# Log-softmax over 50000 columns: loads and stores of a DMA-bound kernel moved from two queues into one, in turns

## The chip, the cores and the metric

The kernel runs on 1 core of one Trainium2 chip. The metric is the device time of one execution in microseconds; medians of several runs are given. A run that lies over 1.5% above the fastest of its kernel is counted as slow; all runs quoted are fast ones unless it is said.

A core has five engines that run instructions (TensorE, VectorE, ScalarE, GpSimd, SyncE) and 16 DMA engines that move data between HBM and the on-chip memory. A DMA issued here by SyncE or by ScalarE is cut into rows and dealt over all 16 DMA engines: the trace of the kernel before has 128 rows and 16 semaphore writes for each transfer. Each issuer has its own queue, q1 and q10 in the profile; a queue's work for one DMA engine is called its ring.

## The reference

```python
x = np.random.randn(16, 512, 50000).astype(np.float32)
max_x = np.max(x, axis=-1, keepdims=True)
shifted = x - max_x
log_sum_exp = np.log(np.sum(np.exp(shifted), axis=-1, keepdims=True))
return (shifted - log_sum_exp).astype(np.float32)
```

1638 MB are read and as many written, once each; the arithmetic is light.

## The kernel before

The 8192 rows are taken 16 at a time: 512 tiles of 128 partitions, where 8 partitions share a row and each holds 6250 numbers (25000 B). A tile is 3.2 MB and stays in one of 8 buffers from its load, through its computation, to its store. A round is 8 tiles. Each tile goes through VectorE (maximum over the partition, four small operations that combine 8 partitions), ScalarE (exponentials with their sums, in two instructions), TensorE (sums over 8 partitions), ScalarE (logarithm), and VectorE again (the subtraction, in place).

SyncE issues the loads. ScalarE issues the stores, each after the exponentials of the next tile:

```python
    @block.sync
    def _(sync):
        for j in range(NBUF):
            sync.dma_start(out=bufs[j], in_=dram(xq, 0, j)).then_inc(landed[j], 16)
        with sync.Fori(1, rounds) as q:
            for j in range(NBUF):
                take(sync, stored[j])          # wait until the buffer's store has landed
                sync.dma_start(out=bufs[j], in_=dram(xq, q, j)).then_inc(landed[j], 16)
        ...
    @block.scalar
    def _(scalar):
        ...
        def back(q, j):
            subtracted.next(                   # wait until VectorE has subtracted
                scalar.dma_start(out=dram(oq, q, j), in_=bufs[j])
            ).then_inc(stored[j], 16)
        ...
        with scalar.Fori(1, rounds) as q:
            last = q - 1
            for j in range(NBUF):
                front(j)                       # exponentials and logarithm of tile j
                back(q if j else last, (j - 1) % NBUF)
            settle()
```

## Time and profile before

| | kernel before |
|---|---|
| median time, 6 runs | 7618.52 us (7617.37 to 7620.07) |
| busy: VectorE, ScalarE, TensorE | 73%, 41%, 7% |
| DMA | 430 GB/s in the mean |

The page's busy digits are tenths of 40 equal slices of the span. The prediction shows the other lines, and uses a finer record, the 16 arrivals at a transfer's semaphore. They are called arrivals below too; a transfer has landed with the last of them.

### The profile page before, as it was taken

To read this page: it belongs to the slowest core of one execution; us is meant where nothing else is said; L and a number is where in the kernel's file an instruction comes from. 1 tells how busy PE (TensorE), PEld (TensorE's weight loads), DVE (VectorE), ACT (ScalarE), POOL (GpSimd) and SP (SyncE) were. 2 spreads that over 40 slices of the span, in tenths; PEclk is the share of its full clock that TensorE was granted. 3 is DMA by queue.
4 is the path that set the end of the run, shared out by engine and by line. 5 is a ranking of instruction groups with operands and counts; after the bars stand their busy time and mean duration, and the time that the engine had idled before them with its cause. 6 is when DMAs were issued, how large, how long until landed. Compare 5 with 4: busy or idle time off the path is not lost. (4 is left out here: it accounts for less than half of the span.)

```text
span 7617.7 us, 14954 instructions
## 1 busy us (share of the span) xinstructions
PE 519.0 (7%) x2048; PEld 475.1 (6%) x2048; DVE 5565.8 (73%) x3072; ACT 3153.3 (41%) x2561; POOL 1.2 (0%) x7
## 2 busy tenths in 40 slices
PE   0000000000000000000000000000000000000000
PEld 0000000000000000000000000000000000000000
DVE  7777777777777777777777777777777777777776
ACT  4444444444444444444444444444444444444443
POOL 0000000000000000000000000000000000000000
DMA  9999999999999999999999999999999999999998
GB/s 424 432 433 432 432 432 432 433 432 432 432 433 433 432 432 432 433 432 432 432 432 433 432 432 432 433 433 432 431 432 433 432 432 432 432 432 432 431 430 366
DMA packets 147459, 3276.88 MB, mean 430 GB/s; under 512 B 16385, under 2 KB 16385, under 8 KB 16385
## 3 DMA queue, kind: packets, MB, share of 16 engines
q1 hardware_dynamic: 73728, 1638.43, 50.0%
q10 hardware_dynamic: 73728, 1638.43, 50.0%
q14 instruction: 3, 0.02, 0.0%
HBM read 1638.40 MB, written 1638.40 MB: 430 GB/s over the span
## 5 line engine op out<-in xcount | busy, mean ns | idle before, releaser
L143 DVE TENSOR_REDUCE pmax<-buf 128x1 f32<-128x6250 f32 x512 | 3411.5, 6663 | 1960.6 <-DVEq L43 1960.6
L190 ACT ACTIVATE dump<-buf,negmax 128x3125 f32<-128x3125 f32 x1024 | 2938.2, 2869 | 3878.6 <-DVE negmax L160 3862.1
L164 DVE TENSOR_SCALAR buf<-buf,negmax,logsum 128x6250 f32<-128x6250 f32 x512 | 1789.4, 3495 | 3.9 <-ACT logsum L197 3.9
L227 PE MATMUL rowsum<-part,ones 128*128 128x1 f32 x2048 | 519.0, 357 | 7078.5 <-ACT dump L190 7078.5
L227 PEld LDWEIGHTS rowsum<-part,ones 128*128 128x128 f32 x2048 | 475.1, 322 | 7122.2 <-ACT dump L190 7122.2
L197 ACT ACTIVATE logsum<-rowsum 128x1 f32<-128x1 f32 x512 | 87.6, 171 | 564.8 <-PE rowsum L227 564.8
L190 ACT ACTIVATION_READ_ACCUMULATOR dump<-buf,negmax 128x1 f32 x1024 | 190.8, 186 | 0.0
L160 DVE STREAM_TRANSPOSE negmax<-spread 128x32 f32<-128x32 f32 x512 | 108.3, 212 | 17.7
L146 DVE STREAM_TRANSPOSE allmax<-pmax 128x32 f32<-128x32 f32 x512 | 108.3, 211 | 17.6
L149 DVE TENSOR_REDUCE rowmax<-allmax 128x4 f32<-128x32 f32 x512 | 95.1, 186 | 17.7
L155 DVE COPY spread<-rowmax 128x32 f32<-128x32 f32 x512 | 92.5, 181 | 17.8
L209 ACT ACT_TABLE_LOAD x1 | 1.3, 1283 | 1.0 <-SPq L90 1.0
L119 POOL TENSOR_SCALAR_AFFINE_SELECT ones<-ones 128x128 f32<-128x128 f32 x1 | 0.4, 403 | 0.1
L123 POOL TENSOR_SCALAR_AFFINE_SELECT ones<-ones 128x128 f32<-128x128 f32 x1 | 0.4, 397 | 0.1
L118 POOL MEMSET ones<- 128x128 f32 x1 | 0.2, 204 | 0.5 <-SPq L90 0.5
L254 POOL MEMSET const-bfloat16-1.0<- 128x1 bf16 x1 | 0.1, 101 | 0.0
L254 POOL MEMSET const-uint8-127<- 128x1 uint8 x1 | 0.1, 101 | 0.0
L254 POOL MEMSET const-float32-0.0<- 128x1 f32 x1 | 0.1, 98 | 0.3 <-issue 0.3
L254 POOL MEMSET const-float32-1.0<- 128x1 f32 x1 | 0.1, 98 | 0.0
## 6 DMA issues: line engine op xcount, KB each, us to landing
buf<-in_x_dram SPq DMA_DIRECT2D x512, 3125.0 KB, 51.8
out_dram<-buf ACTq DMA_DIRECT2D x512, 3125.0 KB, 37.0
```

Source lines behind the costliest of these rows:

```text
L119: gpsimd.affine_select(out=ones3, in_=ones3, pattern=[[-G, R], [0, G]], base=0, channel_multiplier=1, compare_op=ALU.is_ge, fill=0.0,).wai ...
L123: gpsimd.affine_select(out=ones3, in_=ones3, pattern=[[G, R], [0, G]], base=G - 1, channel_multiplier=-1, compare_op=ALU.is_ge, fill=0.0,) ...
L143: vector.reduce_max(out=pmax, in_=bufs[j], axis=AX).then_inc(on_dve.sem)
L146: vector.transpose(out=allmax, in_=pmax.to_broadcast([P, SQ]))
L149: vector.tensor_reduce(out=rowmax, in_=allmax.rearrange("p (r g) -> p r g", g=G), op=ALU.max, axis=AX, negate=True,)
L155: vector.tensor_copy(out=spread.rearrange("p (r g) -> p r g", g=G), in_=rowmax[:, :, None].to_broadcast([P, SQ // G, G]),)
L160: on_dve.next(vector.transpose(out=shift[j], in_=spread)).then_inc(shifted.sem)
L164: vector.tensor_scalar(out=bufs[j], in0=bufs[j], scalar1=shift[j][:, 0:1], scalar2=logs[j], op0=ALU.add, op1=ALU.subtract,)
L190: ins = scalar.activation(out=dump, in_=bufs[j][:, c * EXP_C : (c + 1) * EXP_C], func=ACT.Exp, bias=shift[j][:, 0:1], scale=1.0, accum_out ...
L197: scalar.activation(out=logs[j], in_=rowsum[:, j : j + 1], func=ACT.Ln)
L209: nc.scalar.preload_act_table_set("natural_log_exp_and_others")
L227: ins = tensor.matmul(rowsum[:, j : j + 1], ones, parts[j][:, c : c + 1], start=c == 0, stop=c == nexp - 1,)
```

## The change

The intent: one queue for everything. SyncE issues a store, then a load, then a store, so that loads and stores take turns by whole transfers. Three other stores stand between a buffer's store and the load that fills it again, so that the wait for that store should be over by the time SyncE comes to it. ScalarE is rid of DMA.

```diff
+    LEAD = 3
     @block.sync
     def _(sync):
+        def load(j, src):
+            sync.dma_start(out=bufs[j], in_=src).then_inc(landed[j], 16)
+        def store(j, dst):
+            subtracted.next(sync.dma_start(out=dst, in_=bufs[j])).then_inc(stored[j], 16)
         for j in range(NBUF):
-            sync.dma_start(out=bufs[j], in_=dram(xq, 0, j)).then_inc(landed[j], 16)
+            load(j, dram(xq, 0, j))
+        for j in range(LEAD):
+            store(j, dram(oq, 0, j))
+        subtracted.settle(sync)
         with sync.Fori(1, rounds) as q:
+            last = q - 1
             for j in range(NBUF):
+                k = (j + LEAD) % NBUF
+                store(k, dram(oq, last if k >= LEAD else q, k))
                 take(sync, stored[j])
-                sync.dma_start(out=bufs[j], in_=dram(xq, q, j)).then_inc(landed[j], 16)
+                load(j, dram(xq, q, j))
+            subtracted.settle(sync)
+        for j in range(LEAD, NBUF):
+            store(j, dram(oq, rounds - 1, j))
     ... (ScalarE: back() and its calls removed; its loop now runs from round 0)
```

More of the change, by code (lines that the diff above doesn't have):

```diff
@@ L198, in front @@
             ).then_inc(logged.sem)
-        def back(q, j):
-            subtracted.next(
-                scalar.dma_start(out=dram(oq, q, j), in_=bufs[j])
-            ).then_inc(stored[j], 16)
         def settle():
-            for count in (on_act, shifted, added, subtracted):
+            for count in (on_act, shifted, added):
                 count.settle(scalar)
         nc.scalar.preload_act_table_set("natural_log_exp_and_others")
-        for j in range(NBUF):
-            front(j)
-            if j:
-                back(0, j - 1)
-        settle()
-        with scalar.Fori(1, rounds) as q:
-            last = q - 1
+        with scalar.Fori(0, rounds):
             for j in range(NBUF):
                 front(j)
-                back(q if j else last, (j - 1) % NBUF)
             settle()
-        back(rounds - 1, NBUF - 1)
     @block.tensor
```

## The prediction

> **What bounds the kernel now.** I read the page first, then the stretches at the start and the end, then the timeline of the middle, and last the landing records of single transfers. From the page of the kernel before, the DMA row, the rate row, the queues, and the issues:
>
> ```profile
> DVE  7777777777777777777777777777777777777776
> ACT  4444444444444444444444444444444444444443
> DMA  9999999999999999999999999999999999999998
> GB/s 424 432 433 432 432 432 432 433 432 432 432 433 433 432 432 432 433 432 432 432 432 433 432 432 432 433 433 432 431 432 433 432 432 432 432 432 432 431 430 366
> ...
> q1 hardware_dynamic: 73728, 1638.43, 50.0%
> q10 hardware_dynamic: 73728, 1638.43, 50.0%
> ...
> buf<-in_x_dram SPq DMA_DIRECT2D x512, 3125.0 KB, 51.8
> out_dram<-buf ACTq DMA_DIRECT2D x512, 3125.0 KB, 37.0
> ```
>
> The reader is to see that the 16 DMA engines are full in every slice but the last, that VectorE and ScalarE are not, and that loads (queue q1, from SyncE) and stores (q10, from ScalarE) each take half of the DMA time. A load takes 51.8 us to land and a store 37.0 us, though 3.2 MB at 432 GB/s is 7.4 us: they stand in backlogs, which says that the engines never look for work.
>
> The middle of the kernel (timeline) shows the period of one tile:
>
> ```profile
> 3806.29 6.66 DVE L143 TENSOR_REDUCE pmax<-buf 128x1 f32<-128x6250 f32 x1 [3.84 <-DVEq L43]
> 3806.35 0.34 ACTq L202 DMA_DIRECT2D out_dram<-buf  x1
> ...
> 3821.17 6.66 DVE L143 TENSOR_REDUCE pmax<-buf 128x1 f32<-128x6250 f32 x1 [3.87 <-DVEq L43]
> ```
>
> One tile per 14.88 us here; VectorE works 11.0 us of it (6.66 maximum, 0.9 four small operations, 3.50 subtraction) and waits 3.8 us for its load's landing.
>
> The end looks as if it held a gain. In stretches of 5 us (columns: stretch, its us, the five engines' busy time, clock, DMA share, GB/s):
>
> ```profile
> 7545.00:7550.00 5.00, 0.00 (x0) 0.00 (x0) 4.00 (x5) 4.25 (x3) 0.00 (x0) 1.00 0.96 415
> 7550.00:7555.00 5.00, 1.01 (x4) 0.93 (x4) 2.04 (x1) 1.91 (x3) 0.00 (x0) 1.00 0.42 175
> 7555.00:7560.00 5.00, 0.00 (x0) 0.00 (x0) 4.93 (x3) 0.00 (x0) 0.00 (x0) 1.00 0.95 405
> 7560.00:7565.00 5.00, 0.00 (x0) 0.00 (x0) 3.90 (x4) 4.38 (x3) 0.00 (x0) 1.00 0.23 100
> ```
>
> From 7550 us on the mean share falls to about half, yet VectorE still gets its last tiles only at 7567.8 and 7582.7 us. The share is a mean over 16 engines, so I looked at the 16 arrivals that each transfer's semaphore records, one for each DMA engine. Of the last load, 15 arrive from 7543.9 to 7545.8 us and one at 7582.7. That one falls behind steadily: 1.1 us behind the median in round 3 (a round is 8 tiles), 10.0 in round 21, 18.6 in round 39, 37.5 in round 63. From round 3 to 63 the last arrival advances by 118.94 us a round, so 7.434 us a transfer; the median of the others, from round 3 to 39, by 118.46 us, 7.404 a transfer. **One slow DMA engine bounds the kernel.** Its first load lands at 11.26 us and its last store at 7616.46; 7605.2 us over the 1023 transfers between is 7.434 each, its steady pace. So it has no hole, not even in the tail; the holes are those of the 15 others. In the records a row of 25000 B takes 928 ns in the median and a semaphore write 9 ns: 8 x 928 + 9 = 7433 ns, the slow engine's pace with no gap.
>
> **What the Trainium skill says.** All from "DMA: Bandwidth & Descriptors". "Issuing engines are not separate DMA queues" says that transfers from SyncE and ScalarE run on the same 16 DMA engines and interleave, so that spreading saves only sequencer time. The trace agrees: both queues have 50.0%. "Queues, rings and completion order" says that each issuer has one ring on each DMA engine, that an engine takes turns between rings packet by packet, and that within a ring descriptors are consumed in order. Hence the change replaces alternation by row with alternation by whole transfer. The trace agrees as far as it can: while both queues are full, each takes twice the 7.43 us per transfer. "Why a DMA increments its semaphore by 16 and not by 1" says that the participating engines each post their own arrival; this is what I used above, and the 16 arrivals are there. "Bandwidth", under "Where 436 GB/s comes from", puts the ceiling at 435.2 GB/s. An estimate from that page: 3276.88 MB / 435.2 GB/s = 7529.6 us, 1.2% under the present time. The trace never holds more than 433 in a slice.
>
> **The change, part by part.**
>
> Bytes, transfers and rows are unchanged: 512 loads and 512 stores, 128 rows of 25000 B each.
>
> ScalarE loses 512 issues of 0.34 us, 174 us of its sequencer, and a wait for the subtraction. It is 41% busy and not the bound: worth 0. A store is no longer held until ScalarE is done with the next tile. In the middle, the subtraction that starts at 3813.81 us ends at 3817.31, its store goes out at 3821.18: 3.9 us earlier now. With a backlog in the ring that shortens no transfer: 0.
>
> SyncE gains those issues: two of about 0.33 us in 14.87 us. Worth 0, unless its order blocks it. Its queue is now store of tile n (five turns after its load), load, store, load. In slots of 7.43 us, a load in slot 1 has its store in slot 10, so 8 slots or 59.5 us lie between the load's end and its store's start. What must fit: the landing (about 1.4 us, as the second-last store took 8.8 us from issue to landing for 7.4 us of data); the next load 14.87; its maximum and small operations 7.5; the subtraction 3.5; about 1.5 for issue and first data. That is 29 us of 59.5. In the other direction, a load waits for a store with six transfers behind that store in the ring: 44.6 us of work, against about 3 us for the receipt and the new issue; even where the store before it waited for its subtraction, the load reaches the ring about 5 slots, 37 us, ahead. So the ring never runs dry, and the buffers are not the bound.
>
> The pace in one ring is the open term. The four first loads, alone in their ring, land at 11.26, 18.65, 26.05 and 33.51 us: 7.417 us each, semaphore included, and the late engine falls no further behind in them (0.39 us throughout). The two last stores, also back to back in one ring, land 7.43 us apart (7606.49 and 7613.92 in the median). So neither load after load nor store after store opens a hole for the completion write. A load and a store together make 14.847 us, 7.4235 in the mean. The sum, if changing direction costs nothing: 11.3 to the first landing + 1023 x 7.4235 = 7594.3, + 1.2 from the last landing to the end = 7606.8 us, 11 us less than now.
>
> **The rivals.**
>
> Nothing moves: the late engine is slow in itself, and keeps 7.434 us. Then 11.3 + 1023 x 7.434 + 1.2 = 7617.5 us. For it: it is one engine, always behind. Against it: it did not fall behind while only loads ran, though over 22 us I would see only 0.09 us.
>
> The late engine is slow because of taking turns, and one ring cures it: all go at 7.404, and it is 11.3 + 7574.3 + 1.2 = 7587 us. For it: the loads alone. Against it: the 15 others take the same turns without loss.
>
> The slow engine's extra 0.03 us comes on top of the pace of unmixed transfers: 1023 x 0.03 = 31 us on 7606.8, 7638 us.
>
> A new hole: with one ring an engine has nothing else to do while a transfer's completion is ordered behind its last write or its direction changes. Each 0.05 us in each of 1024 transfers is 51 us: 7658 us with that. Being over 2% slower (152 us) needs 0.15 us a transfer. For it: before, the other ring stood ready just there, and no place of this trace has a load and a store in turns in one ring. Against it: the two pairs of equal kind have no hole.
>
> A dry ring: the wait for another store blocks SyncE, with a ready store behind it. Half a slot lost per tile would be 512 x 3.7 = 1900 us. The 37 us of slack speak against it.
>
> **Range and chances.** I take the middle between "nothing moves" and "pace of unmixed transfers": 7612 us. The cured engine sets the low end, 7582 with a little margin; the high end holds a hole of 0.05 us: 7662. Faster by over 2% would be below 7466 us, under the 7529.6 of the page's ceiling: 0.01. Slower by over 2% needs the hole of 0.15 us or a dry ring, which the trace of before can't exclude: 0.04. Within 2%: 0.95.
>
> **What would show it right or wrong.** The changed profile should have one hardware queue with about 100% of the DMA share; the DMA row at 9 and about 432 GB/s through the middle; VectorE waiting on landings for some 3.8 us per tile; no more 0.34 us issues on ScalarE; a tile period of 14.80 to 14.90 us. Loads should take about 45 us to land or less, stores about 40: in one ring each waits its turn. If the last arrival still falls 0.48 us a round behind the others, the slow engine is slow in itself; if it stays with them, taking turns was to blame. The prediction is wrong if the DMA share sinks in the middle, if rows take visibly over 928 ns or holes follow the 4 B semaphore writes, or if SyncE's wait for a subtraction ends long after the ring is dry.

## The result

| | before | changed |
|---|---|---|
| median of 6 runs | 7618.52 us | 7639.27 us (7638.04 to 7640.7) |
| ratio | | 1.0027, 95% interval 1.0014 to 1.004 |
| span of the profiled run | 7617.7 us | 7637.1 us |

The changed kernel is 0.3% slower: small, but 21 us, where the six runs of each kernel lie within 3 us.

From the page of the changed kernel, the lines that answer to those of before:

```profile
DVE  7777777777777777777777777777777777777776
ACT  4344444444444444444444444444444444444443
DMA  9999999999999999999999999999999999999998
GB/s 419 429 430 431 431 430 431 430 431 431 431 431 431 431 431 431 431 431 431 431 431 431 431 431 431 431 431 431 431 431 431 431 431 431 431 431 431 431 431 371
...
q1 hardware_dynamic: 147456, 3276.87, 100.0%
...
buf<-in_x_dram SPq DMA_DIRECT2D x512, 3125.0 KB, 47.8
out_dram<-buf SPq DMA_DIRECT2D x512, 3125.0 KB, 41.0
```

One hardware queue now has all of the DMA time. The engines are as full as they were, yet the rate is 431 where it was 432 or 433, and 419 to 430 in the first slices. So the time did not go into idle DMA engines: the same rows take longer.

The timeline of the middle:

```profile
3810.20 0.34 SPq L139 DMA_DIRECT2D out_dram<-buf  x1
3810.80 0.35 SPq L136 DMA_DIRECT2D buf<-in_x_dram  x1
...
3814.05 6.66 DVE L163 TENSOR_REDUCE pmax<-buf 128x1 f32<-128x6250 f32 x1 [3.87 <-DVEq L43]
...
3828.93 6.66 DVE L163 TENSOR_REDUCE pmax<-buf 128x1 f32<-128x6250 f32 x1 [3.87 <-DVEq L43]
```

The store is issued as soon as its subtraction ends, the load 0.6 us after it, and VectorE waits for its landing as long as before. The wait of SyncE for the older store costs nothing that can be seen: of the 0.6 us the store's own issue takes 0.34. Over the whole run that wait is 32.8 us; the lines are shown at e4.

The end, in stretches of 5 us as before:

```profile
7565.00:7570.00 5.00, 1.01 (x4) 0.93 (x4) 1.97 (x1) 1.99 (x3) 0.00 (x0) 1.00 0.98 420
7570.00:7575.00 5.00, 0.00 (x0) 0.00 (x0) 4.93 (x3) 0.00 (x0) 0.00 (x0) 1.00 1.01 435
7575.00:7580.00 5.00, 0.00 (x0) 0.00 (x0) 3.97 (x4) 4.31 (x3) 0.00 (x0) 1.00 0.76 325
...
7625.00:7630.00 5.00, 0.00 (x0) 0.00 (x0) 0.00 (x0) 0.00 (x0) 0.00 (x0) 1.00 0.06 25
```

DMA share 0.06 is one engine of 16: the slow one works alone from 7625 us on, at the very end. Its last load arrives at 7598.26 us, and its five last stores at 7605.75, 7613.27, 7620.81, 7628.27 and 7635.74, without a hole. (Arrivals are given from the start of the span, as in the profile. The prediction's are 0.15 us later throughout, which changes none of its differences.)

The arrivals give the account. I take the pace in us for a load and a store together, from the loads of buffer 0 over whole rounds; "median" is the median of the 16 DMA engines, "last" the latest of the 16:

| kernel, rounds | median engine | last engine |
|---|---|---|
| before, 20 to 40 | 14.807 | 14.867 |
| changed, 1 to 8 | 14.901 | 14.947 |
| changed, 20 to 40 | 14.850 | 14.898 |

In rounds 1 to 8 of the changed kernel the buffers differ, from 14.908 to 14.947 on the last engine; from round 20 on they agree.

On the last engine, the first load to the last store took 7616.31 - 11.11 = 7605.2 us before and 7635.74 - 11.09 = 7624.65 us after: 19.45 us more, which is the 19.4 us by which the profiled spans differ. Load for load, the changed kernel is 1.8 us later in round 8 and then falls back by 0.24 us a round, to 15.0 us in round 63. The other 4 us show in the last stores: before, a store ran beside the last load and landed 4.0 us after it; now the first of the five stores that are left lands 7.5 us after it. In the row records the mean row of 25000 B went from 928.7 to 931.6 ns. Before, 96% of the rows took exactly 928 ns; after, 50% did, and most of the others 929 to 941.

The backlog is healthy. Taking, at each issue, the time until the transfer ahead of it in the ring has landed on the last engine, it is never under 33.2 us from the fourth round on, up to the last four stores, which wait for the computation and still find 11.4 us or more. So the ring does not run dry on the engine that bounds the kernel.

### The profile page after: what moved, and what is told of

Read it like the earlier page. It is cut to its first block, busy times and chain, and to the rows that moved or that the text cites. A ratio compares the mean times of both kernels' runs of the same rounds, so it can differ in the third digit from the quotient of the medians.

```text
span 7637.1 us, 14641 instructions
## 1 busy us (share of the span) xinstructions
PE 518.8 (7%) x2048; PEld 474.9 (6%) x2048; DVE 5566.3 (73%) x3072; ACT 3153.3 (41%) x2561; POOL 1.2 (0%) x7
## 6 DMA issues: line engine op xcount, KB each, us to landing
buf<-in_x_dram SPq DMA_DIRECT2D x512, 3125.0 KB, 47.8
```

## The experiments

The theories at the start. **Own pace**, later called **unmixed**: loads alone and stores alone have paces of their own, which are a little worse than both together, and the order in one ring makes each engine do one kind at a time. Rivals: **price of a change**, a small cost each time a ring changes direction; **one ring**, small holes in a ring that a second ring fills; and SyncE's waits.

### Loads alone, stores alone (e1, e2)

```diff
# e1: no compute; 8 stores at the end
-                k = (j + LEAD) % NBUF
-                store(k, dram(oq, last if k >= LEAD else q, k))
-                take(sync, stored[j])
+                take(sync, landed[j])
                 load(j, dram(xq, q, j))
# e2: no compute; 8 loads at the start
-                k = (j + LEAD) % NBUF
-                store(k, dram(oq, last if k >= LEAD else q, k))
                 take(sync, stored[j])
-                load(j, dram(xq, q, j))
+                store(j, dram(oq, q, j))
```

> 512 loads back to back in one ring, no compute, 8 stores at the end (output wrong on purpose). Theory 'own pace' (a direction left to itself has a pace of its own, and changing direction costs nothing): the 15 quick DMA engines take about 7.417 us a load, as the four first loads of the kernel before did; time 11.3 + 511 x 7.417 + 8 x 7.43 + 2 = 3863 us. Theory 'price of a change' (rows of one kind run as quickly as in the kernel before, and each change of direction in a ring costs some 20 ns): 7.404 us a load on the quick engines. If the slow engine is slow in itself, it falls behind by about 0.03 us a load here too, 15 us over the run, and the time is about 3878 us; if only taking turns with stores makes it slow, it stays level.

> 8 loads, then 512 stores back to back in one ring, no compute (output wrong on purpose). 'Own pace': about 7.432 us a store on the quick engines, so that load and store together make the 14.849 us that they take in the changed kernel (118.78 us a round / 8); time 11.3 + 519 x 7.43 + 2 = 3870 us, or 3885 with a slow engine. 'Price of a change': 7.404 us a store, and load and store together 14.81, the kernel before's.

Measured: e1 3868.9 us, e2 3900.0 us (2 runs each; outputs wrong). From the two pages, e1 first, then e2:

```profile
HBM read 1638.40 MB, written 25.60 MB: 430 GB/s over the span
```

```profile
HBM read 25.60 MB, written 1638.40 MB: 427 GB/s over the span
```

With an engine's whole time spent on one kind, the rates are 430 and 427 in spans that include start and end. The arrivals over rounds 20 to 40: a load takes 7.425 us on the median engine and 7.426 on the last; a store 7.447 on the median and 7.487 on the last. Together 14.872 and 14.913. The changed kernel has 14.850 and 14.898, the kernel before 14.807 and 14.867. So unmixed transfers are slower than mixed ones without any change of direction, which is what "own pace" says, by even more than the change lost. "Price of a change" foretold 7.404 us for each kind, and falls. "Own pace" was right in kind and too low in size: it had 7.417 and 7.432 us, and the times came out 6 us (e1) and 15 us (e2, with a slow engine) over its own.

A second thing: in e1 no engine falls behind (the last is 0.4 us behind the median in the last round), in e2 one does, by 0.040 us a store, 20 us at the end. **Left to one kind, an engine is slow in stores only.** Its 0.040 us would make most of the 0.05 to 0.06 us a tile that one engine loses in both whole kernels, if that is the same engine: the records don't number the engines.

The word "median" hides something in e2. The 16 engines have three paces there (rounds 20 to 60): eight take 7.438 us a store, seven 7.456, and one 7.487; 7.447 is only the middle between the first two groups. In e10 below, on another chip (the record has chip 4 for e2 and chip 10 for e10), the groups and their paces are the same within 0.001 us. So it is no fault of one chip. Why the engines fall into these groups is not shown.

### Two stores, then two loads (e3)

```diff
-            for j in range(NBUF):
-                k = (j + LEAD) % NBUF
-                store(k, dram(oq, last if k >= LEAD else q, k))
-                take(sync, stored[j])
-                load(j, dram(xq, q, j))
+            for j in range(0, NBUF, 2):
+                for i in (j, j + 1):
+                    k = (i + LEAD) % NBUF
+                    store(k, dram(oq, last if k >= LEAD else q, k))
+                for i in (j, j + 1):
+                    take(sync, stored[i])
+                    load(i, dram(xq, q, i))
```

> The changed kernel with two stores, then two loads in the ring instead of one and one: half as many changes of direction. 'Own pace': same as the changed kernel, 7639 us within 3. 'Price of a change': half of the 21 us comes back, about 7629 us.

Measured: 7720.17 us (7698.16 to 7735.3, 4 runs), ratio 1.0123. Neither theory foretold that. It goes against "price of a change" in sign, but "own pace" missed it too. The page shows when it happens:

```profile
GB/s 417 424 427 429 431 431 430 430 431 431 431 430 431 431 431 430 430 430 430 429 428 429 430 429 429 426 420 419 416 416 418 417 418 418 418 420 418 414 414 369
```

For some 4000 us it runs nearly at the changed kernel's pace (14.925 us a tile on the last engine in rounds 20 to 40), then drops to 15.32 in rounds 40 to 63. By then the slow engine is 22 us behind. SyncE can only reuse a buffer when the slow engine is done with it, and this order has less in the ring: the last engine's backlog at issue is 28 us in the median, and never under 22.7. The quick engines have that much less the lag. From round 50 on, 12% of the issues reach a median engine whose last transfer landed less than 2 us later, so it is dry or nearly so; in the changed kernel there is none before the last stores. Rows over 950 ns, 1119 in the changed kernel, are 6875 here. That the quick engines come to the edge of running dry is shown. Why the slow engine, with over 20 us of work in its ring, becomes slower at the same time is not, and so it is not shown either that the dryness costs the 1%.

### A shorter lead (e4)

```diff
-    LEAD = 3
+    LEAD = 1
```

> The changed kernel with one other store between a buffer's store and its next load instead of three. The ring's order by kind is the same; a load has 2 transfers (15 us) instead of 6 queued behind the store that it waits for. 'Own pace' and 'price of a change' both say 7639 us within 5. If instead SyncE's waits add to the time, as a third theory says, the shorter slack makes it clearly slower, 7660 us or more.

Measured: 7644.38 us (7641.51 to 7647.0, 4 runs), ratio 1.0032. That is 5 us more than the changed kernel, just over the 5 that were allowed, and the backlog went from 33 to 14.3 us at the least. In rounds 20 to 40 the last engine's pace is again 14.898 us, and the 5 us come from the start (15.085 in rounds 1 to 8 for buffer 0, against 14.947). What SyncE waited for changed altogether. Its waits for a store to land, first in the changed kernel, then in e4 (us in total, times, longest):

```profile
SPq L43 <- SPq L43: 32.8, 6, 8.3
```

```profile
SPq L43 <- SPq L43: 6981.0, 509, 30.1
```

Two hundred times the wait for 5 us: SyncE's waits are not the cause of the 21 us, and three stores of lead are more than enough. In rounds 20 to 40 the median engine, too, takes 14.896 us here, so the quick engines are held back to the slow one's pace, and the slow one loses nothing by it. Held-back quick engines alone do not explain e3.

### Smaller pieces, in one ring or two (e5 to e8)

```diff
# e5: each transfer as two of 64 rows, SyncE;  e7: as eight of 16 rows
-            sync.dma_start(out=bufs[j], in_=src).then_inc(landed[j], 16)
+            for h in PIECES:
+                sync.dma_start(out=bufs[j][h], in_=src[h]).then_inc(landed[j], 16)
# e6: rows 0 to 63 from SyncE, rows 64 to 127 from ScalarE, between its own work, loads four tiles ahead
# e8: store piece, load piece, store piece, load piece ... in one ring
```

> Control. The changed kernel with each transfer issued as two of 64 rows, both from SyncE, in the same order of kinds (two half stores, two half loads). Same rows, one more semaphore write of 9 ns for each half load and half store: 2 x 9 ns x 512 = 9 us. All theories: 7639 + 9 = 7648 us, within 8.

> As e5, but the second half of each transfer is issued from ScalarE: two rings in turns on each DMA engine, both of which hold stores and loads in the changed kernel's order, so an engine still has one kind at a time. Theory 'unmixed' (what the changed kernel loses is that an engine no longer has loads and stores in flight at once): as e5, within 8 us. Theory 'one ring' (a single ring has small holes that a second ring fills): the kernel before's pace, some 20 us under e5, about 7628 us.

> Control. The changed kernel with each transfer issued as eight of 16 rows, one row for each DMA engine, all eight of a store and then all eight of a load, from SyncE. 14 more semaphore writes of 9 ns per tile: 65 us. All theories: about 7704 us, or more if small transfers cost more than their semaphore write.

> As e7, but the 16-row stores and 16-row loads take turns one by one in the single ring: an engine changes direction after each row, as in the kernel before, with one ring as in the changed kernel. 'Unmixed': 15 to 20 us under e7. 'One ring': as e7. 'Price of a change', which e3 already speaks against: 16 times as many changes of 20 ns, more than 100 us over e7.

Measured, all with correct results, medians of 4 runs: e5 7742.99, e6 8985.21, e7 9120.21, e8 11981.92 us. (Two of e6's runs and one of e7's are counted as slow; e6's fast ones are 8835.45 and 8872.14 us.) The controls e5 and e7 missed their own numbers by 95 and 1416 us, so the four can't answer the question that they were made for. What went wrong is in the first stretches, where only loads run (columns as before; e5, then e7):

```profile
4.00:12.00 8.00, 0.00 (x0) 0.00 (x0) 0.00 (x0) 0.00 (x0) 0.00 (x0) 1.00 1.06 222
12.00:20.00 8.00, 0.00 (x0) 0.00 (x0) 0.43 (x1) 0.00 (x0) 0.00 (x0) 1.00 0.97 203
```

```profile
12.00:20.00 8.00, 0.00 (x0) 0.00 (x0) 0.00 (x0) 0.00 (x0) 0.00 (x0) 1.00 0.86 100
20.00:28.00 8.00, 0.00 (x0) 0.00 (x0) 0.00 (x0) 0.00 (x0) 0.00 (x0) 1.00 0.89 103
```

Loads of 64 rows run at half of the 432 GB/s of 128 rows, loads of 16 rows at a quarter. The Trainium skill, "SBUF — State Buffer", section "Door 1: The DMA port swizzle", says that the rate depends on how many of 16 ports the partitions reach, and by its table 64 consecutive partitions reach 8 and 16 consecutive ones 4. These rates agree with it. Later the DMA engines get out of step (in e5 the arrivals at one buffer spread over 9.0 us in the first round and 19.8 in the next) and e5 recovers to about 430 GB/s: its first slice of 40, at 248 GB/s, holds some 80 of the 95 us. But the pieces are spoilt as a test: I changed how the rows lie on the ports together with what I wanted to change. Little can be kept. The pair e7 and e8 has the same pieces, and taking turns row by row in one ring took 2862 us more than eight and eight. But with one and the same order e8 runs at 422 GB/s in one slice and at 217 in another, so no price of a single change of direction can be read from it. Why e6, with the pieces of e5 in two rings, took over 1000 us more than e5 is not explained either.

### One kind in two rings (e9, e10)

The clean form of the question whether the second ring matters: e1 and e2 again, whole transfers, dealt in turn to both queues.

```diff
+    @block.sync
+    def _(sync):
+        half(sync, range(0, NBUF, 2))      # the same loop, even tiles
+    @block.scalar
+    def _(scalar):
+        half(scalar, range(1, NBUF, 2))    # odd tiles
```

> e1 with the tiles dealt in turn to SyncE's and ScalarE's rings (512 loads, whole transfers, no compute, output wrong on purpose). Two rings in turns, but still one kind at a time. 'One ring': the rows go back to 928 ns, as they were with two rings in the kernel before, and a load takes 7.404 us instead of the 7.425 of e1: 11 us less than e1, about 3858 us. 'Unmixed': as e1, 3869 us within 4.

> e2 with the tiles dealt in turn to the two rings (512 stores, output wrong on purpose). 'One ring': the mean row falls from 934 to 928 or 929 ns and the time by 20 to 30 us, to about 3875 us. 'Unmixed': as e2, 3900 us within 5, with one engine still about 0.04 us a store behind the others.

Measured: e9 3868.09 us (e1 3868.9), e10 3900.3 us (e2 3900.0), 2 runs each. The pace on the median and the last engine is 7.425 and 7.425 us a load, 7.447 and 7.488 us a store; the mean rows are 931.1 and 934.1 ns, where they were 931.0 and 934.2. A second ring does nothing for transfers of one kind, though in e9 the row after a row on an engine always comes from the other queue. "One ring" falls; what the kernel before has and these have not is loads beside stores.

### Relieving the slow engine (e11)

```diff
# kernel before; tile 0 of rounds 8, 24, 40 and 56, and the matching wait for 32
-        scalar.dma_start(out=dst, in_=bufs[j]).then_inc(stored[j], 16)
+        scalar.dma_start(out=dst[:120], in_=bufs[j][:120]).then_inc(stored[j], 16)
+        scalar.dma_start(out=dst[120:], in_=bufs[j][120:]).then_inc(stored[j], 16)
```

The rule meant below is in "DMA: Bandwidth & Descriptors" of the Trainium skill, section "Why a DMA increments its semaphore by 16 and not by 1": a transfer issued by SyncE or ScalarE uses the largest number of engines up to 16 that divides its slowest dimension on both sides, and takes the lowest-numbered ones.

> The kernel before, except that in 4 of the 64 rounds one store is issued as 120 rows and 8 rows, which by the Trainium skill's rule on how many engines a transfer uses should leave out DMA engine 15 for the 120 (8 rows for each of 15 engines) and engines 8 to 15 for the 8. If the engine that falls behind is number 15, it is relieved of 4 x 8 rows, 29.7 us, of the 31 us that it falls behind in the whole run (512 x 0.06), the pace is that of the others, 14.807 us a tile, and the time is 11.3 + 512 x 14.807 + some 5 = about 7595 us, the first version under the kernel before. If it is one of 8 to 14, nothing changes (7618); if one of 0 to 7, it has 4 rows more, and it is 7622 us.

Measured: 7729.44 us (7637.59 to 7766.05, 6 runs, two of them counted as slow), ratio 1.0144; none of the three numbers came. The profiled run, 7637.59 us, is the best. The trace agrees with the rule on the number of engines: it has 28 semaphore writes more than the kernel before, 7 for each of the 4 split stores, as 15 + 8 - 16. In the stores of round 9, after the first such store, one engine arrives 16.5 us ahead of the median, and another is still 4.6 us behind and goes on falling behind, to 7.4 in round 15. So an engine was relieved, and not the one that falls behind. Besides, each such store costs something itself: the last engine's pace for the loads, 14.86 us in round 7, is 15.17 in round 9 and 15.74 in round 25. So if the page's numbering holds, the slow engine is not number 15; which one it is stays open, and so does the scatter of this version's runs.

### Both kinds in both rings (e12)

```diff
# even tiles: loads and stores from SyncE; odd tiles: from ScalarE; order in each ring as in the changed kernel
-    subtracted = Count(sem("subtracted"))
+    subtracted = [Count(sem("subtracted_even")), Count(sem("subtracted_odd"))]
...
+            store(k, dram(oq, last if k else q, k))   # SyncE, even k = j + 2
+            take(sync, stored[j])
+            load(j, dram(xq, q, j))
```

> The changed kernel's order by turns, but with the even tiles' loads and stores in SyncE's ring and the odd tiles' in ScalarE's (whole transfers; each ring has store, load, store, load, with one other store of its own between a buffer's store and its next load). Two rings, each of both kinds. 'One ring' (e9 and e10 speak against it): the kernel before's 7618 us within 5, whatever the phases. 'Unmixed': it depends on what stands beside what, which the landings will show. Where both rings hold the same kind at a time, the changed kernel's pace, 14.90 us a tile on the slow engine, 7637 us; where a store runs beside a load, the kernel before's 14.87 and 7620 us; a mixture lies between. A dry ring, which the shorter lead could bring, would show as rows over 950 ns and 7660 us or more.

Measured: one run of 7630.96 us, five of 7816.92 to 7846.13 us; the five are counted as slow by their distance from the first, and the profile is of that kind, with 10154 rows over 950 ns and the median engine 27 us ahead of the last. That looks like the dry ring of e3 again, on the quick engines, so the profile says nothing on the pace, and the single quick run, between the two kernels, has no trace. Inconclusive.

No version with right results beat the kernel before.

## Why the prediction was right, and where it was off

**The bound.** It named one slow DMA engine as what bounds the kernel, without a hole in its work. That held: the change in this engine's time from first to last arrival, 19.45 us, is the whole change of the span. In the changed kernel, too, the half-empty DMA row near the end is that of the quick engines.

One proof that it offered does not hold. "8 x 928 + 9 = 7433 ns, the slow engine's pace with no gap" is a coincidence: 928 ns is the row of the quick engines as well, which are at 7404. In the records a row starts 3.3 ns in the mean before the one ahead of it on its engine ends, so that eight rows and a semaphore write take 7433 - 9 x 3.3 = 7403 ns, the quick engines' pace. The slow engine's rows must be longer; its last three, stores at the very end of the kernel before, took 941, 941 and 932 ns.

"Alternation by row" in the kernel before was its own step, too: the section that it names says packet, typically of several descriptors. The row records bear it out: where rows can be put to engines by their times, 87% of rows (1000 to 6000 us) follow one of the other queue.

**ScalarE's and SyncE's parts, each worth 0.** Right. ScalarE's issues are gone and the stores go out right after their subtraction, and the time did not fall. SyncE's issues take 0.34 and 0.35 us.

**The slack.** The prediction had a load reach the ring some 37 us ahead; the backlog at issue is 37.0 us in the median and 33.2 at the least. E4 shows that less than half of it would do. The rival "dry ring" did not come true here. E3, where the quick engines are nearly dry and 1% is lost, may be a case of it.

**The signs.** Most came: one queue with 100.0%, the DMA row at 9, 431 GB/s for 432, a wait of 3.87 us on VectorE, a period of 14.88 us. The loads took longer to land than foretold (47.8 us, where it said about 45 or less), the stores 41.0 for about 40. The last arrival still falls behind, by 0.38 us a round (8 x 0.048), which it took as the sign of an engine that is slow in itself. But one of its own signs of being wrong came as well: rows over 928 ns. Half of them are, the mean being 931.6, and this is the loss.

**The pace in one ring, the open term.** The central time, 7612 us, was 27 us too low. The measured time lies in the range because the high end left room for a hole of 0.05 us, and no such hole came: the range was right in part by luck. The sum itself, 7606.8 us, lies 30 us under the profiled span of 7637.1, and the runs show where. Its pace of 14.847 us for a load and a store was nearly that of the median engine in the changed kernel, 14.850: 2 us over 512 tiles. (This is luck in part: it came from four loads and two stores at the two ends of the trace. Over 512 of each, e1 and e2 have 7.425 us for 7.417 and 7.447 for 7.43, in sum 14.872, and the kernel stays below that.) What the sum left out is the slow engine: 14.898 us a tile on the last engine, 0.048 above the median, 25 us over 512 tiles. The rest, some 4 us, is at the start and the end. The third rival, "the slow engine's extra 0.03 us comes on top of the pace of unmixed transfers", 7638 us, is what happened, with 0.024 us a transfer instead of 0.03. The step that failed is the choice to "take the middle between 'nothing moves' and 'pace of unmixed transfers'", rather than to add the slow engine's part to the latter. The argument that the slow engine did not fall behind in the first loads was sound as an observation, and e1 confirms it over 512 loads; but it was taken as a doubt whether the engine is slow in itself. By e2 the loss is in the stores, which those first loads couldn't show.

**What stays open.** The changed kernel's pace lies 0.015 to 0.022 us a tile under the sum of e1 and e2. A likely reason is that its engines are some us out of step, so that some store while others load; the first rounds, with the engines more in step, are slower (14.947 for buffer 0) than the later ones. That is argued, not shown: 14.947 is also above 14.913, the sum of e1 and e2, so the start has a cost of its own, and e12, which could have shown the mixing inside the kernel, failed. Whether the loss arises in each DMA engine or on a path that all share is open for the same reason, and so is why one engine is slow in stores.

## What to carry to other kernels

When the DMA engines are full, look at the arrivals of single transfers and not only at the mean share: the last engine sets the time, and a half-empty row at the end may be the others waiting for it. Where the transfers are long and the DMA engines are the bound, try loads and stores side by side, one queue for each, before one queue in turns: in this kernel the single queue cost 0.3%, though the DMA engines stayed full and VectorE waited no longer for a tile. When you cut a transfer for an experiment, check first that the pieces alone still run at full rate.

## What the Trainium skill lacked or had wrong

- "DMA: Bandwidth & Descriptors", "Issuing engines are not separate DMA queues", says that spreading transfers over issuers saves only sequencer time. For transfers of one kind this holds to 1 us in 3900 (e1 and e9, e2 and e10). It lacks that a mixture is quicker: 14.867 us on the last engine for a load beside a store in two queues, 14.913 for the same two alone (e1 plus e2), 14.898 in turns in one queue.
- The same page, under "Where 436 GB/s comes from", says that for transfers between HBM and SBUF the HBM side binds, at some 358 GB/s. The sentence lacks its condition, which the page gives elsewhere: that share is for both cores of a pair streaming. With one core at work these kernels held 431 to 433 GB/s for reads and writes together, near the page's other figure of 435.
- No page that I read has DMA engines that differ in stores alone. Here the 16 had three paces in stores, 7.438, 7.456 and (one engine) 7.487 us per 3.2 MB, and one pace in loads, 7.425 (e2, e1). The DMA page, under "Latency and other measured facts", has engines 7 and 15 as usually slower and ties that, as a best guess, to transfers issued by GpSimd, of which there are none here.
